# A feed-forward block with its down projection turned round: tokens stand, weight columns move

## Chip, cores and metric

The kernel runs on one core of a Trainium2 chip. The metric is the device time of one execution in microseconds (us); less is better. The number given is the median of several executions.

## What is computed

One layer of a hybrid decoder for 320 tokens (256 of a new sequence, 8 x 8 of running ones), width 2048. Two token mixers (an mLSTM and an HGRN2) are merged and projected, and a feed-forward block follows. Inputs and weights are fp32. The part that matters here:

```
x1 = LayerNorm(alpha * x + mix)                      # alpha = 2 ** 0.25
hid = square(relu(x1 @ w_up))                        # w_up (2048, 8192)
y  = LayerNorm(alpha * x1 + hid @ w_down)            # w_down (8192, 2048)
```

The recurrent states of both mixers are outputs too.

## The kernel before

**Split products.** Every fp32 operand is split into a high half (the value rounded to the matmul's fp32r format, a ScalarE copy) and a low half (the rest, a VectorE subtraction). A product is three matmuls into one PSUM bank: high x high, high x low, low x high.

**Tiles and units.** All large projections have one form: a tile is 128 output columns; its weights stand in the array (128 x 128 pieces) and the 320 tokens move past them. A tile of 2048 input rows comes in two units of 1024 rows (`UNITS`), each one load of 512 KB into one of three raw buffers (`wr`), one ScalarE instruction for the high half and one VectorE instruction of 128 x 1024 for the low half (`prep`, L520). Halves lie in buffers `wh`/`wl` (three pairs), from the output projection on in four more that lie in tile `bb`. A unit gives TensorE 8 x 3 = 24 matmuls of 320 columns. Results are transposed: channels on partitions, tokens along the row.

**Order.** `tile_list` fixes the order of the tiles. The feed-forward part goes in four rounds f: 16 tiles "up" (2048 hidden channels), then 16 tiles "dn" that multiply these by their 2048 rows of `w_down`; each dn tile is added to `acc` (`ev_dn`, L2070, L2073). Up tiles of round 0 start before the first LayerNorm is known: they use unnormalised x1 and `ev_up` corrects the result afterwards (L2052, L2054), while `x1` (L2023, L2024) writes the normalised rows; in the first dn round `xs_` splits these for the later up rounds (L1778 into `xl`). Hidden channels are split into `bah`/`bal`.

**Who decides what runs when.** The program is written out by a planner (`Sched`): each chain of work is a generator, and the planner keeps one clock per engine, with a cost for each instruction, and emits the next instruction of the most urgent chain that would be ready. So the order on each engine is fixed when the program is built; on the chip an engine waits, in that order, for semaphores. All loads and stores but a few go over SP's queue.

**Last norm and end.** Sums over channels are matmuls with ones (`ln_add`, `total`, `ln_final`), since channels lie on partitions. After the last dn tile `y` normalises 16 tiles of 128 x 320 (L2090, L2097, one ScalarE instruction each) and stores them, while TensorE makes the final states (`m_C`: 48 matmuls of 512 columns; `h_S`: 16 products of 256 columns) from copies that POOL's queue and SP's queue bring back from memory.

Of the kernel before, what the change touches and what calls it, by code (L numbers as in the profile page):

```python
# [39 lines left out]
def tile_list():  # L40
# [34 lines left out]
UNITS = [(i, half) for i in range(FIRST, len(TILES)) for half in range(2)]  # L75
# [215 lines left out]
PE_T = 112.0  # L291
PE_4 = 400.0
# [40 lines left out]
class Program:  # L333
    def __init__(self, tc, nc, d, pools):
# [16 lines left out]
        self.f2 = p.tile([128, 5204], F32, name="f2")  # L351
        self.f3 = p.tile([128, 5120], F32, name="f3", tag="f3")
        self.rx = p.tile([128, 4096], F32, name="rx", tag="rx")
# [28 lines left out]
    def carve(self):  # L382
# [28 lines left out]
        X = Part(self.rx)  # L411
        self.cb = Pool([C(512) for _ in range(6)] + [X(512) for _ in range(8)])
# [36 lines left out]
    def carve_h(self):  # L449
# [7 lines left out]
        rxb = self.pool.tile([128, 4096], F32R, name="rxb", tag="rx")  # L457
        X, R, V, W, Z = self.Part(rxb), self.Part(self.ra), self.Part(self.ra), self.Part(rxb, 2880), self.Part(rxb, 3840)
        self.nc.gpsimd.memset(rxb[:, 3840:4096].bitcast(F32), 0.0)
        self.halves = Pool([(V(512), V(512), W(448), W(448))])  # L460
        self.vp = Pool([V(256), rxb[:, 2624:2880]])
        self.ats = Pool([(Z(128), Z(128))])
        self.bah = Slices([(X if j < 12 else R)(TOK) for j in range(KT)])
# [8 lines left out]
    def carve_m(self):  # L472

        f3 = self.pool.tile([128, 5120], F32, name="f3m", tag="f3")
        self.acc = self.mm_ = self.Part(f3).three(KT, TOK)
        self.ln[0]["z"], self.ln[1]["z"] = self.mm_, self.acc

    def carve_x(self):

        self.sx = []  # L480
        for name, n in (("xh", 6), ("xl", 2)):
            R = self.Part(self.pool.tile([128, KT * (TOK + 2)], F32, name=name + "s", tag=name))
            self.sx += [R(768) for _ in range(n)]

    def carve_o(self):
        R = self.Part(self.pool.tile([128, 4096], F32, name="oC", tag="rx"))
        self.oC = [R.three(2, 512) for _ in range(MH)]
        self.oS = self.Part(self.pool.tile([128, 6656], F32, name="oS", tag="ra")).three(HH, 256)
# [12 lines left out]
    def prep(self, must=False):  # L501

        u = self.next_prep
        if u >= len(UNITS) or not self.hl_free:
            return False
        now = self.s.t["pe"]
        if must:
            self.s.until(lambda: u in self.raw_at)
        elif u not in self.raw_at:
            return False  # L510
# [1695 lines left out]
```

## Time and profile before

| | |
|---|---|
| median of 3 runs | 2276.83 us (2276.64 to 2277.16) |
| profiled execution, span | 2275.6 us, 39057 instructions |
| TensorE (PE) busy | 2267.5 us, 100% |
| VectorE (DVE) busy | 1392.1 us, 61% |
| ScalarE (ACT) busy | 1170.8 us, 51% |
| moved by DMA | 424.95 MB, 187 GB/s |

The span is the time between the first and the last instruction of the profiled execution; the median of the runs lies 1.2 us above it. "PE" are matmuls, "PEld" the loading of the standing operand, which overlaps them; "PEclk" is the clock granted to TensorE, in tenths of full speed or as a fraction. Matmuls are pipelined: one of 320 columns is listed with some 309 ns, but the next starts sooner. In lists of groups the columns are line, engine, operation, tiles, shapes and count, then busy us and mean ns, then idle time before them and what ended it. In an order of time the columns are start, duration, what.

### The profile page before, as it was taken

To read this page: it belongs to the slowest core of one execution; us is meant where nothing else is said; L and a number is where in the kernel's file an instruction comes from. 1 tells how busy PE (TensorE), PEld (TensorE's weight loads), DVE (VectorE), ACT (ScalarE), POOL (GpSimd) and SP (SyncE) were. 2 spreads that over 40 slices of the span, in tenths; PEclk is the share of its full clock that TensorE was granted. 3 is DMA by queue.
4 is the path that set the end of the run, shared out by engine and by line. 5 is a ranking of instruction groups with operands and counts; after the bars stand their busy time and mean duration, and the time that the engine had idled before them with its cause. 6 is when DMAs were issued, how large, how long until landed. Compare 5 with 4: busy or idle time off the path is not lost.

```text
span 2275.6 us, 39057 instructions
## 1 busy us (share of the span) xinstructions
PE 2267.5 (100%) x15518; PEld 2230.4 (98%) x15518; DVE 1392.1 (61%) x2426; ACT 1170.8 (51%) x2081; POOL 12.5 (1%) x36
## 2 busy tenths in 40 slices
PE   9999999999999999999999999999999999999998
PEld 9999999999999999999999999999999999999998
DVE  5676777777777777666555767544444444444456
ACT  6566555678777766444433446533432343234334
POOL 0000000000000000000000000000000000000000
PEclk9999999999999999999999999999999999999999
DMA  7588898666666575555556544444444444444476
GB/s 283 175 266 253 277 285 248 211 191 189 188 195 211 178 216 175 175 173 172 172 173 198 193 153 147 148 150 151 153 148 148 149 151 153 150 148 148 150 229 194
DMA packets 227438, 424.95 MB, mean 187 GB/s; under 512 B 96436, under 2 KB 122932, under 8 KB 226232
## 3 DMA queue, kind: packets, MB, share of 16 engines
q1 hardware_dynamic: 222376, 415.98, 56.9%
q0 software_dynamic: 4736, 6.29, 1.2%
q8 instruction: 121, 1.98, 0.4%
q14 instruction: 61, 0.50, 0.1%
q10 hardware_dynamic: 144, 0.20, 0.0%
HBM read 371.49 MB, written 50.90 MB: 186 GB/s over the span
## 4 chain that ended last, share of the span: by engine, by line
PE 97%; ACT 2%; DVE 0%; issue 0%; ACTq 0%; POOL 0%; DVEq 0%; POOLq 0%
PE bank L375 97%; ACT f L369 1%; ACT wh L369 0%; ACT f3m L369 0%; ACT ra L369 0%; ACT oC L369 0%; DVE f3m L2090 0%; DVE f3m L2097 0%; DVE wl L520 0%; ACT oS L369 0%; ACT xh L369 0%; ACTq L2202 0%; ACT f3h L369 0%; DVE f L1975 0%; DVE f L1974 0%
## 5 line engine op out<-in xcount | busy, mean ns | idle before, releaser
L520 DVE TENSOR_TENSOR wl<-wr,wh 128x1024 fp32r<-128x1024 f32 x440 | 538.8, 1225 | 432.3 <-ACT wh L369 429.2
L375 PE MATMUL bank<-xh,wh 128*128 128x320 f32 (+1 forms) x2504 | 786.5, 315 | 0.0
L375 PE MATMUL bank<-xh,wl 128*128 128x320 f32 (+1 forms) x2504 | 774.4, 310 | 0.0
L375 PE MATMUL bank<-xl,wh 128*128 128x320 f32 (+1 forms) x2504 | 772.1, 309 | 0.0
L369 ACT ACTIVATE wh<-wr 128x1024 fp32r<-128x1024 f32 x440 | 465.4, 1058 | 456.1 <-PE bank L375 437.0
L375 PEld LDWEIGHTS bank<-xh,wh 128*128 128x128 f32 x2504 | 471.2, 188 | 9.2 <-issue 7.3
L375 PEld LDWEIGHTS bank<-xl,wh 128*128 128x128 f32 x2504 | 471.3, 188 | 3.0
L375 PEld LDWEIGHTS bank<-xh,wl 128*128 128x128 f32 x2504 | 471.6, 188 | 0.2 <-DVE wl L520 0.2
L369 ACT ACTIVATE bb<-wr 128x1024 fp32r<-128x1024 f32 x162 | 171.6, 1059 | 296.0 <-PE bank L375 276.0
L520 DVE TENSOR_TENSOR bb<-wr,bb 128x1024 fp32r<-128x1024 f32 x162 | 198.5, 1225 | 195.2 <-ACT bb L369 195.0
L375 PE MATMUL bank<-ra,wh 128*128 128x320 f32 x1008 | 276.2, 309 | 0.7 <-DVE ra L1778 0.7
L375 PE MATMUL bank<-ra,bb 128*128 128x320 f32 x1096 | 255.5, 309 | 0.0
L375 PE MATMUL bank<-xh,bb 128*128 128x320 f32 (+1 forms) x1136 | 253.8, 309 | 0.0
L375 PE MATMUL bank<-rxb,bb 128*128 128x320 f32 x1088 | 249.1, 309 | 0.0
L375 PEld LDWEIGHTS bank<-xh,bb 128*128 128x128 f32 x1136 | 191.0, 188 | 0.0
L375 PE MATMUL bank<-rxb,wl 128*128 128x320 f32 x608 | 187.9, 309 | 0.0
L375 PE MATMUL bank<-rxb,wh 128*128 128x320 f32 x608 | 187.9, 309 | 0.0
L375 PEld LDWEIGHTS bank<-ra,bb 128*128 128x128 f32 x1096 | 185.2, 188 | 0.0
L375 PEld LDWEIGHTS bank<-rxb,bb 128*128 128x128 f32 x1088 | 184.6, 188 | 0.0
L375 PEld LDWEIGHTS bank<-ra,wh 128*128 128x128 f32 x1008 | 181.3, 188 | 0.9 <-DVE ra L1778 0.9
L375 PE MATMUL bank<-xl,bb 128*128 128x320 f32 (+1 forms) x568 | 175.5, 309 | 0.0
L369 ACT ACTIVATE f<-f 32x128 f32<-32x128 f32 (+6 forms) x405 | 150.7, 373 | 37.1 <-DVE f L1343 19.0
(274 smaller groups left out, 2257.3 us busy)
## 6 DMA issues: line engine op xcount, KB each, us to landing
wr<-wt SPq DMA_DIRECT2D x602, 512.0 KB, 3.4
rx<-C SPq DMA_DIRECT2D x36, 256.0 KB, 5.1
Cs<-rx SPq DMA_DIRECT2D x36, 256.0 KB, 4.5
f<-C SPq DMA_DIRECT2D x28, 256.0 KB, 4.7
Cs<-f SPq DMA_DIRECT2D x28, 256.0 KB, 5.5
f<-first SPq DMA_DIRECT2D x6, 704.0 KB, 9.6
vD<-ra SPq DMA_DIRECT2D x4, 1024.0 KB, 6.5
f<-S SPq DMA_DIRECT2D x8, 512.0 KB, 5.1
```

What stands on the lines that cost most here:

```text
L369: return self.nc.scalar.activation(out, in_, func, **kw)
L375: self.nc.tensor.matmul(*a, **kw)
L520: self.V().tensor_tensor(lo, raw, hi.bitcast(F32), ALU.subtract)
```

## The change

- `tile_list` gives 64 up tiles in eight phases of eight tiles (1024 hidden channels each) and no dn tiles. `unit_list` puts a phase's down units between the up units of the next phase (`merge`): phase 0 starts with five down units, a later one with one; the last phase has down units alone.
- In the down projection the hidden channels of 128 tokens stand and 512 weight columns move. A phase has four pairs of 128 rows; `g` is a half of the 2048 output columns. Phases 0 to 6 use a seven-product form of a 2 x 2 block product (tokens 0-127 and 128-255, the two row blocks of a pair, the two column blocks of a half): unit A and B make 10 matmuls, C 9, into three banks each (`PASSES`). The last 64 tokens stand with high and low halves side by side, two matmuls instead of three. The last phase is plain (units D and E, 16 matmuls each).
- `highs` and `lows` replace `prep` from the first down unit on. B adds two weight blocks, C forms three sums from two loads and has a third block of halves. A down unit's weights are loaded once for A or B and again for C: 8 x 4 x 7 loads for A, B and C, 16 for D and E. `refill` hands a raw buffer to the next load; `carve_dn` adds a fourth raw buffer, in the scratch tile of the first norm.
- `ev_up` leaves hidden channels in fp32, `operands` makes the differences (`Z`) and splits them. `ev_block` keeps 18 blocks of 128 x 512 and adds each phase to them; `residual` combines these after phase 6 and adds alpha * x1, which `spill_x1` has transposed and stored after phase 0's start.
- Tokens now lie on partitions, so the last norm takes its statistics along rows (`ev_last`, `norm`); gain and bias are loaded as rows. The output is stored as 12 pieces of up to 128 x 512, and the states in 16 stores.
- Buffers `rx`, `f2` and others are cut differently.

```
-    for f in range(4):
-        t += [("up", j, f, "w_up", 0, (f * 16 + j) * 128) for j in range(16)]
-        t += [("dn", j, f, "w_down", f * D, j * 128) for j in range(16)]
+    t += [("up", j, j // 8, "w_up", 0, j * 128) for j in range(8 * PH)]
     return t
...
+PH, PAIRS = 8, 4
...
+def merge(down, up, lead):
+    out, rest = down[:lead], down[lead:]
+    for n, u in enumerate(up):
+        out.append(u)
+        out += rest[len(rest) * n // len(up):len(rest) * (n + 1) // len(up)]
+    return out if up else down
+def unit_list():
+    w = lambda lo, hi: [("w", i, half) for i in range(lo, hi) for half in range(2)]
+    u = w(FIRST, UP0 + 8)
+    for p in range(PH):
+        kinds = "ABC" if p < PH - 1 else "DE"
+        down = [(k, p, g, i) for g in range(2) for k in kinds for i in range(PAIRS)]
+        u += merge(down, w(UP0 + 8 * p + 8, UP0 + 8 * p + 16) if p < PH - 1 else [], 1 if p else 5)
+    return u
...
+RAWS = dict(w=(None,), A=(0,), B=(1,), C=(0, 1), D=(0,), E=(1,))
...
+PASSES = dict(
+    A=((0, "a", 0), (1, "b", 512), (2, "s", 0), (2, "t", 512)),
+    B=((0, "z7", 0), (1, "z3", 512), (2, "s", 0), (2, "sd", 512)),
+    C=((0, "z5", 0), (1, "d", 512), (2, "z6", 1024)),
+    D=((2, "s", 0), (2, "t", 512), (0, "a", 0), (0, "b", 512), (1, "c", 0), (1, "d", 512)),
+)
+PASSES["E"] = PASSES["D"]
+PARTS = dict(A="AS", B="BS", C="C", D="ASC", E="ASC")
...
+    def carve_dn(self):
+        now = self.s.t["pe"]
+        B = self.Part(self.pool.tile([128, 5204], F32, name="f2m", tag="f2"))
+        self.m_blocks = [B(512) for _ in range(5)] + self.m3
+        self.refill(B(1024), now)
+        self.qp[1].free += [(now, B.three(2, TOK)) for _ in range(2)]
+        self.mbank.free += self.sbank.free
...
+    def refill(self, buf, at):
+        r = self.next_raw
+        if r < len(RAW_UNIT):
+            self.next_raw += 1
+            self.raw[r] = buf
+            self.s.spawn(self.reload(r, at), -2)
...
+    def highs(self):
+        v = self.nc.vector
+        for u in range(U_MLP, len(UNITS)):
+            kind = UNITS[u][0]
+            rs = RAW_OF[u]
+            yield wait(*[self.raw_ev[r] for r in rs])
+            raw = [self.raw[r] for r in rs]
+            buf = yield acq(self.hlp)
+            x = raw[0]
+            if kind == "B":
+                yield ("dve", SUM, lambda: v.tensor_tensor(x[:, 0:512], x[:, 0:512], x[:, 512:1024], ALU.add))
+            if kind == "C":
+                y = raw[1]
+                yield ("dve", SUM, lambda: v.tensor_tensor(x[:, 0:512], x[:, 0:512], y[:, 0:512], ALU.add))
+                yield ("dve", SUM, lambda: v.tensor_tensor(y[:, 0:512], x[:, 0:512], y[:, 512:1024], ALU.add))
+                yield ("dve", SUM, lambda: v.tensor_tensor(x[:, 512:1024], x[:, 512:1024], y[:, 0:512], ALU.add))
+            yield ("act", HI, lambda: self.A(buf[0], x))
+            self.half[u] = [buf, None]
+            yield post(self.hi_ev[u])
+            if kind == "C":
+                c2 = yield acq(self.c2)
+                yield ("act", act(512), lambda: self.A(c2[:, 0, :], y[:, 0:512]))
+                self.half[u][1] = c2
+                yield post(self.h2_ev[u])
+    def lows(self):
+        v = self.nc.vector
+        for u in range(U_MLP, len(UNITS)):
+            yield wait(self.hi_ev[u])
+            raw = [self.raw[r] for r in RAW_OF[u]]
+            hi, lo = self.half[u][0]
+            x = raw[0]
+            t = yield ("dve", LO, lambda: v.tensor_tensor(lo, x, hi.bitcast(F32), ALU.subtract))
+            self.refill(x, t)
+            if UNITS[u][0] == "C":
+                yield wait(self.h2_ev[u])
+                c2, y = self.half[u][1], raw[1]
+                t = yield ("dve", SUM, lambda: v.tensor_tensor(c2[:, 1, :], y[:, 0:512], c2[:, 0, :].bitcast(F32), ALU.subtract))
+                self.refill(y, t)
+            self.unit[u] = (self.half[u][0], t + LAT)
...
+    def down(self, u, kind, p, g, i):
+        s = self.s
+        if (kind, g, i) == ("A", 0, 0) and p == 0:
+            s.until(lambda: self.n_zg == 8 and all(e.t is not None for e in self.acc_ev))
+            self.carve_dn()
+            s.spawn(self.xs_(), 0)
+            s.spawn(self.spill_x1(), 4)
+        if (kind, g, i) == ("D", 0, 0):
+            self.carve_end()
+            ...
+            s.spawn(self.residual(), 1)
+        if (kind, g, i) == ("E", 1, 0):
+            for j in range(MH):
+                s.spawn(self.m_C(j), 3)
+            for j in range(HH):
+                s.spawn(self.h_S(j), 3)
+        if i == 0:
+            self.banks = [self.take() for _ in range(3)]
+        (hi, lo), at = self.halves_of(u)
+        c2 = self.half[u][1]
+        X = self.X[p, i]
+        for part in PARTS[kind]:
+            s.until(lambda: X["ev" + part].t is not None)
+            at = max(at, X["ev" + part].t + LAT)
+        s.t["pe"] = max(s.t["pe"], at)
+        passes = PASSES[kind]
+        for n, (b, name, o) in enumerate(passes):
+            wh, wl = (c2[:, 0, :], c2[:, 1, :]) if o == 1024 else (hi[:, o:o + 512], lo[:, o:o + 512])
+            x = X[name]
+            jobs = [(x[0], wh), (x[1], wh), (x[0], wl)] if len(x) == 2 else [(x[0], wh), (x[0], wl)]
+            for m, (l, w) in enumerate(jobs):
+                self.mm(self.banks[b], l, w, start=..., stop=...)
+                s.t["pe"] += 227.0
+            if i == PAIRS - 1 and n == last[b]:
+                s.spawn(self.ev_block(kind, p, g, b, self.banks[b]), 0)
+        self.give(u)
...
+    def spill_x1(self):
         v = self.nc.vector
+        for j in range(KT):
+            yield wait(self.xs_ev[j])
+            z = self.mm_[:, j, :]
+            yield ("dve", dve_t(TOK), lambda: v.transpose(z, z))
+            yield from self.place(lambda a: cap2(self.xD, 128 * j + 32 * a, [[D, 32], [32 * D, 10], [1, 32]]),
+                                  z.rearrange("p (b c) -> p b c", c=32))
+        yield wait(self.later())
+        self.carve_f3()
+        yield post(self.f3_ev)
...
+    def ev_up(self, T, p, b):
+        v = self.nc.vector
+        i, h = T % 8 // 2, T % 2
+        if h == 0:
+            self.Q[p, i] = yield acq(self.qp[p > 0])
+            yield post(self.q_ev[p, i])
+        else:
+            yield wait(self.q_ev[p, i])
+        q = self.Q[p, i][:, h, :]
+        if p:
+            yield ("act", act(TOK, True), lambda: self.A(q, b[:, :TOK], AF.Relu))
             yield rel(self.mbank, b)
+        else:
+            sm = yield acq(self.sm)
+            yield ("act", act(2, True), lambda: self.A(sm[:, 0:2], b[:, TOK:TOK + 2]))
+            yield wait(self.ln[0]["end"])
+            yield ("dve", dve(TOK, True), lambda: v.scalar_tensor_tensor(q, self.lnb[3], sm[:, 0:1], b[:, :TOK], ALU.mult, ALU.subtract))
+            yield rel(self.mbank, b)
+            yield ("dve", dve(TOK), lambda: v.tensor_tensor(q, q, self.lnb[4], ALU.mult))
+            yield ("act", act(TOK, False, 1), lambda: self.A(q, q, AF.Relu, scale=-1.0, bias=sm[:, 1:2]))
+            yield rel(self.sm, sm)
+            self.n_zg += 1
+        yield ("act", act(TOK), lambda: self.A(q, q, AF.Square))
+        yield post(self.hq_ev[T])
+        if h:
+            yield wait(self.hq_ev[T - 1])
+            yield from self.operands(p, i)
...
+    def operands(self, p, i):
...
+        if not plain:
+            Z = yield acq(self.zp)
+            yield ("dve", dve(256), lambda: v.tensor_tensor(two(Z, 0, 128, 128), two(flat, 0, 128, 128), two(flat, 128, TOK, 128), ALU.subtract))
+            yield ("dve", dve(128), lambda: v.tensor_tensor(Z[:, 384:512], Z[:, 0:128], flat[:, TOK + 128:TOK + 256], ALU.add))
+            yield ("dve", dve(128), lambda: v.tensor_tensor(Z[:, 256:384], Z[:, 384:512], flat[:, TOK:TOK + 128], ALU.subtract))
+            yield ("dve", dve(64), lambda: v.tensor_tensor(Z[:, 512:576], flat[:, TOK + 256:2 * TOK], flat[:, 256:TOK], ALU.subtract))
+        A = X["A"] = yield acq(self.pA)
+        yield from halves(two(A, 0, 128, 128), two(A, 256, 128, 128), two(flat, 0, TOK, 128), 256)
+        X["a"], X["b"] = (A[:, 0:128], A[:, 256:384]), (A[:, 128:256], A[:, 384:512])
+        yield post(X["evA"])
...
+    def ev_block(self, kind, p, g, b, bank):
+        v = self.nc.vector
+        if kind in "DE":
+            yield from self.ev_last("DE".index(kind), g, b, bank)
             return
+        if p == 0 and 9 * g + 3 * "ABC".index(kind) + b >= 8:
+            yield wait(self.f3_ev)
+        M = self.block(kind, g, b)
+        if p:
+            yield ("dve", dve(512, True), lambda: v.tensor_tensor(M, M, bank, ALU.add))
+        else:
+            yield ("act", act(512, True), lambda: self.A(M, bank))
+        yield rel(self.mbank, bank)
+        if p == PH - 2:
+            yield post(self.sum_ev[kind, g, b])
...
+    def residual(self):
...
+            yield wait(*[self.sum_ev[k, g, b] for k in "ABC" for b in range(3)])
+            blocks = ((P2, P3), (Q4, P7), (S1, S2))
+            yield tt(P2, P1, P2, ALU.add)
+            yield tt(P1, P1, Q6, ALU.subtract)
+            yield tt(Q6, P1, P7, ALU.add)
+            yield tt(Q4, Q4, Q6, ALU.add)
+            yield tt(Q5, Q5, P1, ALU.subtract)
+            yield tt(P3, Q5, P3, ALU.subtract)
+            yield tt(P7, Q5, P7, ALU.subtract)
+            for n in range(2):
+                c = 2 * g + n
+                for x in range(3):
+                    yield ("dve", SUM, lambda: v.scalar_tensor_tensor(w, e, ALPHA, w, ALU.mult, ALU.add))
+                    yield post(self.w_ev[c][x])
...
+    def ev_last(self, n, g, x, bank):
+        v = self.nc.vector
+        c = 2 * g + n
+        W = self.last(c, x)
+        yield wait(self.w_ev[c][x])
+        yield ("dve", dve(512, True), lambda: v.tensor_tensor(W, W, bank, ALU.add))
+        yield rel(self.mbank, bank)
+        rows = 128
+        if x == 2:
+            t = yield acq(self.ts)
+            rows = 64
+            yield ("act", act(512), lambda: self.A(t[0:64], W[64:128]))
+            yield ("dve", SUM, lambda: v.tensor_tensor(W[0:64], W[0:64], t[0:64], ALU.add))
+            yield rel(self.ts, t)
+        yield ("dve", SUM, lambda: v.bn_stats(self.st[:rows, x, c, :], W[:rows]))
+        yield post(self.s_ev[x, c])
+        if c == 3 and x != 0:
+            yield from self.norm((2,) if x == 2 else (0, 1))
...
+    def norm(self, xs):
...
+        for j, x in enumerate(xs):
+            m, r = self.mv[:rows, x, 0:1], sm[:rows, 9 + n + j:10 + n + j]
+            for c in range(4):
+                W = self.last(c, x)[:rows]
+                cc = slice(512 * c, 512 * c + 512)
+                yield ("dve", SUM, lambda: v.scalar_tensor_tensor(W, W, m, G[:rows, cc], ALU.subtract, ALU.mult))
+                yield ("dve", SUM, lambda: v.scalar_tensor_tensor(W, W, r, B[:rows, cc], ALU.mult, ALU.add))
+                yield ("sp", 620, lambda: self.dma(self.d["y"][128 * x:128 * x + rows, cc], W))
```

More of the change, by code (lines that the diff above doesn't have):

```diff
@@ L474, in carve_m @@
         f3 = self.pool.tile([128, 5120], F32, name="f3m", tag="f3")
[L475 to L488, printed above, removed]
+        self.mm_ = self.Part(f3).three(KT, TOK)
@@ new lines, in carve_f3, with carve_end @@
+    def carve_f3(self):
+        m10 = self.Part(self.pool.tile([128, 5120], F32, name="m10", tag="f3"))
+        self.m_blocks += [m10(512) for _ in range(10)]
+    def carve_end(self):
+        R = self.Part(self.pool.tile([128, KT * (TOK + 2)], F32, name="xhe", tag="xh"))
+        self.erest = R.ap
+        self.er = [R(2048), R(2048), R(1024)]
+        R = self.Part(self.pool.tile([128, KT * (TOK + 2)], F32, name="xle", tag="xl"))
+        self.gb2 = [R(2048), R(2048)]
+        self.ts = Pool([R(512) for _ in range(2)])
@@ L708, in start @@
         self.zg_ev = [Ev() for _ in range(KT)]
-        self.hid_ev = [[Ev() for _ in range(KT)] for _ in range(4)]
         self.m_ev = [Ev() for _ in range(KT)]
```

429 lines of the change are left out of this document (248 added, 181 removed).

## The prediction

> **What bounds the kernel now.** I read the page first (busy shares, the slices, the chain), then the chain in order of time, then stretches of the last half, then single instructions.
>
> ```profile
> span 2275.6 us, 39057 instructions
> PE 2267.5 (100%) x15518; PEld 2230.4 (98%) x15518; DVE 1392.1 (61%) x2426; ACT 1170.8 (51%) x2081; POOL 12.5 (1%) x36
> ...
> DVE  5676777777777777666555767544444444444456
> ...
> PEclk9999999999999999999999999999999999999999
> ...
> PE 97%; ACT 2%; DVE 0%; issue 0%; ACTq 0%; POOL 0%; DVEq 0%; POOLq 0%
> ```
>
> TensorE is busy all the time at full granted clock and holds 97% of the chain. VectorE (DVE) has room, most of it in the last 900 us, which is the feed-forward part.
>
> ```profile
> 620.43 732.63 PE bank L375 x5053
> 1353.06 111.37 PE bank L375 x750
> ...
> 1468.30 783.58 PE bank L375 x5341
> ```
>
> The last piece is almost the whole feed-forward part: 783.58 / 5341 = 146.7 ns per matmul. So time is the number of matmuls times their spacing, as long as the other engines keep up:
>
> ```profile
> core 0: us, PE busy (x) PEld busy (x) DVE busy (x) ACT busy (x) POOL busy (x), PEclk, DMA share, GB/s
> ...
> 300.00:400.00 100.00, 100.00 (x685) 91.84 (x685) 78.62 (x156) 54.70 (x96) 0.00 (x0) 1.00 0.87 263
> ...
> 700.00:800.00 100.00, 100.00 (x713) 97.60 (x712) 77.20 (x181) 77.15 (x182) 0.37 (x1) 1.00 0.63 188
> ...
> 1470.05:2245.00 774.95, 774.95 (x5289) 774.95 (x5289) 363.93 (x437) 280.32 (x342) 4.87 (x7) 1.00 0.47 153
> 2252.95:2262.48 9.53, 9.53 (x44) 7.88 (x43) 8.85 (x22) 7.30 (x14) 0.00 (x0) 1.00 0.71 272
> 2269.50:2275.60 6.10, 0.04 (x1) 0.00 (x0) 0.42 (x1) 0.76 (x2) 0.00 (x0) 0.81 0.69 241
> ```
>
> VectorE 77% and ScalarE 77% busy (700 to 800 us), or 263 GB/s (300 to 400 us), still left TensorE full; the feed-forward part uses 47% of VectorE and 153 GB/s.
>
> **Matmuls.** The state products behind the last weight tile already run in the new shape, 512 moving columns of split fp32r:
>
> ```profile
> 2252.95 0.84 PE L375 MATMUL bank<-bb,wl 128*128 128x512 f32 x3
> 2253.64 2.20 PE L375 MATMUL bank<-bb,wh 128*128 128x512 f32 x9
> 2255.68 0.84 PE L375 MATMUL bank<-bb,wl 128*128 128x512 f32 x3
> ```
>
> Nine starts take 2255.68 - 2253.64 = 2.04 us: 227 ns each, at granted clock 1.00 (window 2252.95 to 2262.48). Old down projection: 4 x 16 tiles x 16 x 3 = 3072 matmuls x 146.7 = 450.7 us. New: a pair (256 rows of w_down by 1024 columns) takes 10 + 10 + 9 = 29 matmuls in the seven-product form, 7 phases x 2 x 4 x 29 = 1624; the plain phase 2 x 4 x (16 + 16) = 256. 1880 x 227 = 426.8 us: **-23.9 us**. Per pair: 7.04 us before, 6.58 after, plain 7.26, so merely turning the operands costs 3% and the missing product earns it back. The margin is 3.4 us per phase of 109 us; everything below is whether stalls eat it.
>
> The Trainium skill ("TensorE: Matmul & The Clock Gate", Back-to-back issue gap) gives N/2.4 + 2.5 ns, 216 ns for 512 columns, by which the new projection would take 405 us and the gain be 45 us. The same rule gives 136 ns for 320 columns where the trace has 146.7, so the measured 227 decides.
>
> **VectorE per phase** (16 up units with 24 down units, 384 x 146.7 + 232 x 227 = 109.0 us of TensorE). Spacing of instructions back to back:
>
> ```profile
> 1412.74 1.23 DVE L520 TENSOR_TENSOR wl<-wr,wh 128x1024 fp32r<-128x1024 f32 x1 [1.78 <-ACT wh L369]
> 1413.88 0.48 DVE L2023 TENSOR_TENSOR f3m<-f3m,f 128x320 f32<-128x320 f32 x1
> 1414.28 0.49 DVE L1778 TENSOR_TENSOR ra<-f,rxb 128x320 fp32r<-128x320 f32 x1
> ...
> L1305 DVE SCALAR_TENSOR_TENSOR rx<-rx,f,bank 128x512 f32<-128x512 f32 x36 | 25.8, 737 | 0.2
> ...
> L369 ACT ACTIVATE wh<-wr 128x1024 fp32r<-128x1024 f32 x440 | 465.4, 1058 | 456.1 <-PE bank L375 437.0 <-issue 9.6 <-DMA wr<-wt 6.9
> ```
>
> 1024 elements 1.14 us, 320 elements 0.40 us; on the line through both (an estimate) 512 take 0.60, 256 0.33, 128 0.20, 64 0.13. Low halves 40 x 1.14 = 45.6. Sums of weights (one in B, three in C, and C's third low half): 40 x 0.60 = 24.0. Adding banks: 18 x 0.65 (737 less the overlap of 0.09) = 11.7. Operands of four pairs: 4 x (4 x 0.33 + 4 x 0.20 + 2 x 0.13) = 9.5. Together 91 us, 83% of 109. ScalarE has 40 x 0.97 (1058 less the same overlap) plus smaller copies, about 60 us; it does not bind. So TensorE stays the bound on average, but not everywhere: four C units with their 2.8 up units give TensorE 4 x 2.04 + 9.9 = 18.0 us and VectorE 4 x (1.14 + 4 x 0.60) + 3.2 + 2.0 + 1.6 = 20.9 us.
>
> **Weight loads** of the down projection go from 128 to 240, on SP's queue. Issue (0.33 us each) takes 16 us of a phase there:
>
> ```profile
> wr<-wt SPq DMA_DIRECT2D x602, 512.0 KB, 3.4
> ...
> L378 SPq DMA_DIRECT2D wr<-wt x602: 327/328/2364, 9.7 to 2231.2; - x151
> ```
>
> 48 loads per 109 us are 231 GB/s, below the 263 of 300 to 400 us. Four raw buffers (three, and one more from the first down unit on) allow 4 x 109 / 48 = 9.1 us per load. A plain load holds its buffer 3.4 + 1.06 + 1.23 + hand-overs, about 6 us; C's two hold theirs about 9 us each, since three sums stand ahead of the high half. In a C stretch that is 4 x 18.5 + 2.8 x 6 = 91 buffer-us for 72 at hand: 23 us instead of 18, 5 us late, 14 times. The cover is the prepared units: five buffers of halves, four of them ahead at about 2.7 us, 10.9 us; A and B stretches (11.4 and 13.8 us of VectorE for 18.9) refill them. That units are prepared ahead until the buffers are full shows here (waits inside the feed-forward part):
>
> ```profile
> ACT bb L369 <- PE bank L375: 271.3, 128, 2.5
> ACT wh L369 <- PE bank L375: 203.7, 96, 2.5
> DVE bb L520 <- ACT bb L369: 176.4, 136, 2.9
> DVE wl L520 <- ACT wh L369: 134.4, 105, 2.9
> ```
>
> ScalarE waits for TensorE to free a buffer. I take **0** for the C stretches, bounds 0 and 14 x 5 = 70 us.
>
> **Start of the first down phase.** It now comes after 8 up tiles, not 16, and needs every operand that reads the first norm.
>
> ```profile
> 1346.10 0.31 PE L375 MATMUL bank<-xh,bb 128*128 128x322 f32 x1
> ...
> 1364.72 0.49 DVE L1976 SCALAR_TENSOR_TENSOR f<-f 128x320 f32<-128x320 f32 x1
> ...
> L2023 DVE TENSOR_TENSOR f3m<-f3m,f x16: 483/484/487, 1367.0 to 1421.0; 128x320 f32<-128x320 f32 x16
> ...
> L369 ACT ACTIVATE xh<-f3m x16: 453/456/463, 1462.0 to 1490.8; 128x320 fp32r<-128x320 f32 x16
> L1778 DVE TENSOR_TENSOR xl<-f3m,xh x16: 483/485/488, 1463.7 to 1492.1; 128x320 fp32r<-128x320 f32 x16
> ...
> 1468.30 0.41 PE L375 MATMUL bank<-ra,wh 128*128 128x320 f32 x1 [0.65 <-DVE ra L1778]
> ```
>
> The first up tile starts at 1346. The norm ends at 1365 and x1 (L2023) lasted to 1421, hidden under up tiles that ran to 1464. Eight up tiles end at 1346 + 56 = 1402. From 1367 to 1402 VectorE would have 13 us of x1, 7 of evictions, 12 of low halves and 10 of operands, 42 us for 35, plus chained waits: x1 ends near 1412. The split of x1 (16 x 0.9 us, strictly after it) delays the up units of the next phase, which follow only five down units (11.3 us) later: eight splits make 1421, so 1421 - 1402 - 11.3 = **+7.7 us**, and the old gap of 0.65 goes. Bounds: -0.65 (x1 packed tighter) and +20 (x1 at its old pace to 1421, splits behind it). SP's queue waits there too: the fourth raw buffer lies in the norm's scratch, so its first load stands until x1 is done, with the other weight loads behind it; five units of halves are ready by then and cover that. Behind that, 16 transposes and 64 small stores of x1 must end before the ninth block is evicted, some 50 us on; banks give slack for 30 us more. I take **+3**, bounds 0 and 15.
>
> **Tail.**
>
> ```profile
> L1069 DVE BATCH_NORM_STATS2 misc<-f 128x6 f32<-128x512 f32 x12 | 8.3, 688 | 0.9 <-ACT f L369 0.8
> ...
> 2250.46 0.86 PE L375 MATMUL bank<-bb,wh 128*128 128x512 f32 x3
> ...
> 2266.52 1.69 DVE L2097 TENSOR_TENSOR f3m<-f3m,f 128x320 f32<-128x320 f32 x4
> ...
> 2267.65 1.89 PE L375 MATMUL bank<-xls 128*128 128x256 f32 x8
> ...
> 2270.78 0.95 SPq L378 DMA_DIRECT2D Sp<-oS  x2
> ```
>
> Now the last tile ends at 2250.5 and the program 25.1 us later: VectorE 18 us, TensorE's state products 19. Afterwards the same 48 + 16 state products stay; VectorE adds the last bank and two before it and takes their statistics (0.65 + 0.60 each; about 2.5 us are left after the last matmul), forms the root (some seven short instructions and two of ScalarE, taken as 2 us), then 24 instructions of 0.60 = 14.4: 19 us. The outputs go in 28 stores instead of 21 (7 more issues, 2.3 us of SP beside that). The plain phase before it (58.1 us of TensorE) holds 51 us of VectorE: 16 low halves 18.2, the residual 26 x 0.60, twelve additions and statistics with four folds, 17.4. State products' operands come over POOL's queue into buffers freed by the last five units; the order of the state products leaves them 8 us and more. I take **0**, bounds -3 and +5.
>
> **Sum** against the execution's span: 2275.6 - 23.9 - 0.65 + 7.7 + 3 = 2261.8; the median stands 1.2 us above that span (2276.83): **2263**.
>
> **Rivals.**
> 1. Everything hides: start and spill cost nothing. 2276.8 - 24.5 = 2252. For: before, the gap at the same seam was 0.65 us. Against: x1 ended 19 us after the new seam.
> 2. VectorE waits on ScalarE (slower). Before each low half VectorE sat idle 310.8 us / 241 = 1.29 us. Alternating with ScalarE, it keeps some of that idle. The work of a phase is 91 us and about 4 of gaps between dependent sums; at 0.5 us idle for each of 40 units a phase takes 91 + 4 + 20 = 115 instead of 109, +42 over seven: 2263 + 42 = 2305. It decides once the remaining 14 us are gone, 2 us per phase, at 0.4 us idle per unit. For: 83% load, and C above 100%. Against: 77% on both engines together left TensorE full (700 to 800 us), so most idle is slack, not need.
> 3. The C stretches break through in part, 1 us each: 2263 + 14 = 2277, no change.
>
> The clock can fall in the gaps: it reads 0.81 in the idle last 6.10 us, which is worth 0.19 x 6.1 = 1.2 us per gap. The Trainium skill (same page, Part 1) halves it after an idle window of 3.4 us; no gap inside the old feed-forward part was that long, so no run here shows it there.
>
> **How the numbers follow.** Forecast (2256 to 2272) 0.50; all hidden 0.18; no change 0.12; VectorE bound 0.20. Range 2250 to 2300: it leaves out the worse half of the last case and little else; the forecast's own range is 2256 to 2272. A measurement of this kernel tells about 0.2% (2272 to 2281) from no change: faster 0.68, same 0.12, slower 0.20.
>
> **What would show it.** The 512-column matmuls 227 ns apart at clock 1.00; in steady phases VectorE busy 83 to 90% and TensorE full at 109 us per phase, 231 GB/s; TensorE gaps of 4 to 12 us after the eighth up tile, ended by x1's split; a tail of 22 to 30 us. The forecast is wrong if TensorE's waits name a low half of a C unit or a weight load again and again, if the first down phase lasts over 130 us, or if the spacing is not 227 ns.

## Result and the profile after

The kernel became slower: 2340.79 us (2339.35 to 2341.54) against 2276.99 us, a ratio of 1.0279 [1.0264, 1.0294]. The forecast was 2263 us, the range ended at 2300. The profiled execution has a span of 2339.8 us, 64.2 us over the one before.

The page after, its lines that answer to those of before:

```profile
span 2339.8 us, 37835 instructions
PE 2286.6 (98%) x14316; PEld 2142.6 (92%) x14316; DVE 1697.1 (73%) x2982; ACT 1280.9 (55%) x2339; POOL 12.6 (1%) x36
...
DVE  6676677777677876565556688777877787777776
...
PE 24%; DVE 7%; DMA 4%; ACT 3%; issue 2%; SPq 0%; POOL 0%; DVEq 0%; ACTq 0%; POOLq 0%
```

There are 1202 matmuls fewer (1192 in the down projection, and ten with `ones`). The chain can be followed back only to 1411 us here, so its shares add up to some 40% of the span: of the last 929 us TensorE holds some 557 (24% of the span), and loads, VectorE and ScalarE have come into it. The same view in order of time (start, duration, what; some of the longest pieces of one phase) shows where:

```profile
1645.20 41.67 PE bank L411 x231
1693.40 1.24 DVE wl L660
1694.65 3.44 DMA wr<-wd
1703.08 33.81 PE bank L411 x187
1739.44 3.55 DMA wr<-wd
1749.15 3.42 DMA wr<-wd
1762.43 43.22 PE bank L411 x231
```

Before, TensorE held one piece of 783 us. Now it holds some 40 us, the units A and B of a half with their up units, and then the chain leaves it for 16 to 26 us: the C units. By phases (from the first up unit of one to that of the next), behind a row of the start and ahead of one of the tail:

```profile
core 0: us, PE busy (x) PEld busy (x) DVE busy (x) ACT busy (x) POOL busy (x), PEclk, DMA share, GB/s
1403.00:1441.00 38.00, 32.89 (x147) 26.16 (x146) 32.63 (x62) 24.00 (x47) 0.00 (x0) 0.91 0.64 170
1528.73:1649.26 120.53, 114.24 (x617) 101.35 (x616) 92.39 (x137) 57.47 (x88) 0.00 (x0) 0.97 0.64 210
1649.26:1768.03 118.77, 113.61 (x617) 100.75 (x616) 94.63 (x142) 58.74 (x91) 0.00 (x0) 0.99 0.65 217
...
2316.34:2321.60 5.26, 5.26 (x13) 4.10 (x13) 5.12 (x9) 0.60 (x1) 0.00 (x0) 0.50 0.85 317
```

A phase takes 119 to 121 us instead of 109.0, with VectorE busy 92 to 95 us of it. What TensorE waited for between 1530 and 2230 (us in total, times, longest) are halves of units, high and low:

```profile
PE bank L411 <- ACT bb L405: 20.0, 12, 3.4
PE bank L411 <- DVE bb L660: 7.6, 15, 0.5
```

The row of 2316 is in the tail; it is read below.

**Ledger.** From the first up matmul to the last matmul on a weight tile the kernel took 904.4 us before (1346.1 to 2250.5) and takes 953.6 now (1346.0 to 2299.6): +49.2. The tail behind it was 25.1 us and is 40.2: +15.1. The 49.2 are made of -23.9 (matmuls, as forecast at 227 ns), +10.5 (their spacing is 233 ns), some +10 at the start (1402 to 1445) and some +55 behind it, in the C stretches. "Lost" here and below is the length of a stretch less what its matmuls, counted in the trace, need at 147 and 233 ns. Of the 55, 45.5 are in the five phases from 1528.73 to 2125.74, each 9.1 us over what a phase takes with no waits (110.3 us; experiment 3 shows that figure); 2.6 lie before them and 6.4 behind. This adds up to some 52; the ten matmuls with `ones`, which are gone, take off 1.5.

**One C stretch**, second half of phase 2. The chain of waits between 1739 and 1763:

```profile
1739.44 3.55 DMA wr<-wd
...
1743.08 0.69 DVE wr L640
1743.78 0.60 DVE m L2320
1744.37 0.60 DVE wr L641
1744.98 1.19 DVE m L2320 x2
1746.17 0.61 DVE wr L642
...
1746.81 1.07 ACT wh L405
...
1747.90 1.22 DVE wl L660
...
1749.15 3.42 DMA wr<-wd
...
1761.15 1.24 DVE bb L660
...
1762.43 2.75 PE bank L411 x6
```

A load lands; three sums (with additions of banks, L2320, between them), the high half on ScalarE, the low half on VectorE; only then is the buffer given to the next load, which goes out at 1749.15, 9.7 us after the one before. Each link waits for the last. VectorE, in the stretch that was thought its tightest, stands idle for the load:

```profile
1743.08 0.69 DVE L640 TENSOR_TENSOR wr<-wr 128x512 f32<-128x512 f32 x1 [1.46 <-DMA wr<-wd]
...
1752.67 0.69 DVE L640 TENSOR_TENSOR f2m<-f2m,wr 128x512 f32<-128x512 f32 x1 [1.27 <-DMA wr<-wd]
```

The pace is read from the copies into `c`, one for each C unit (minimum/median/maximum ns, first and last start):

```profile
L405 ACT ACTIVATE c<-wr x4: 616/617/621, 1738.2 to 1761.3; 128x512 fp32r<-128x512 f32 x4
```

Three steps in 23.1 us: 7.7 us for each C unit. TensorE needs 9 x 0.233 + 0.7 x 24 x 0.147 = 4.57 us for a C unit with its share of up units (16 stand between 23 down units). So four of them make 4 x (7.7 - 4.57) = 12.5 us of delay. The cover, TensorE's lead at the end of B, was some 8 us: the last B unit has its low half (list of VectorE) ready at 1733.52 + 1.23 = 1734.75, and TensorE takes it up (list of TensorE) at 1742.58:

```profile
1733.52 1.23 DVE L660 TENSOR_TENSOR bb<-wr,bb 128x1024 fp32r<-128x1024 f32 x1 [0.51 <-ACT bb L405]
```

```profile
1742.58 1.57 PE L411 MATMUL bank<-bb,xp 128*128 128x512 f32 x6
...
1757.22 1.21 PE L411 MATMUL bank<-bb 128*128 128x512 f32 x4 [0.51 <-DVE bb L660]
1758.27 0.99 PE L411 MATMUL bank<-c,bb 128*128 128x512 f32 x3
1761.17 0.73 PE L411 MATMUL bank<-bb 128*128 128x512 f32 x2 [1.91 <-ACT bb L405]
1762.43 1.90 PE L411 MATMUL bank<-bb 128*128 128x512 f32 x4 [0.53 <-DVE bb L660]
```

By the third C unit the lead is gone and TensorE waits for each half as it is made. 12.5 - 8 = 4.5 us a stretch, two stretches a phase: 9 us, the loss seen. That it fits so closely is in part luck. The waits of this stretch are 0.51 + 1.91 + 0.53 = 2.95 us, since TensorE begins with a unit's high half before the low half is done (1761.17 and 1762.43); most of the rest is the granted clock, which reads 0.50 from 1762.7 to 1766.1, just behind them. Low clock is in the loss everywhere: 0.97 to 0.99 over the five phases is worth some 12 of the 45.5 us.

### The profile page after: what moved, and what is told of

Same layout as the page of the kernel before. It is cut to its first block, busy times and chain, and to the rows that moved or that the text cites. A ratio compares the mean times of both kernels' runs of the same rounds, so it can differ in the third digit from the quotient of the medians.

```text
span 2339.8 us, 37835 instructions
## 1 busy us (share of the span) xinstructions
PE 2286.6 (98%) x14316; PEld 2142.6 (92%) x14316; DVE 1697.1 (73%) x2982; ACT 1280.9 (55%) x2339; POOL 12.6 (1%) x36
## 5 line engine op out<-in xcount | busy, mean ns | idle before, releaser
L411 PEld LDWEIGHTS bank<-xl,wh 128*128 128x128 f32 x2776 | 522.7, 188 | 11.4 <-DVE xl L1984 4.7
L660 DVE TENSOR_TENSOR bb<-wr,bb 128x1024 fp32r<-128x1024 f32 x89 | 108.8, 1222 | 52.8 <-ACT bb L405 52.5
L405 ACT ACTIVATE f<-f 32x256 f32<-32x256 f32 (+6 forms) x339 | 120.7, 357 | 35.9 <-DVE f L1550 19.0
L411 PE MATMUL bank<-xh,bb 128*128 128x320 f32 (+1 forms) x592 | 136.2, 310 | 0.0
L411 PE MATMUL bank<-ra,wh 128*128 128x320 f32 x468 | 128.3, 309 | 0.0
L411 PE MATMUL bank<-wh,xp 128*128 128x512 f32 x336 | 118.1, 402 | 0.0
L411 PE MATMUL bank<-bb,wh 128*128 128x320 f32 (+1 forms) x524 | 116.7, 312 | 0.0
L411 PE MATMUL bank<-bb 128*128 128x512 f32 x294 | 86.3, 420 | 30.6 <-ACT bb L405 21.7
L411 PE MATMUL bank<-bb,xp 128*128 128x512 f32 x416 | 104.2, 396 | 0.0
L411 PEld LDWEIGHTS bank<-xh,bb 128*128 128x128 f32 x592 | 100.6, 188 | 1.5 <-DVE bb L660 0.2
L411 PE MATMUL bank<-wl,xp 128*128 128x512 f32 x232 | 92.7, 400 | 0.0
```

The source lines that it names most:

```text
L405: return self.nc.scalar.activation(out, in_, func, **kw)
L411: self.nc.tensor.matmul(*a, **kw)
L660: t = yield ("dve", LO, lambda: v.tensor_tensor(lo, x, hi.bitcast(F32), ALU.subtract))
```

## The experiments

Theory 1: the load buffers pace the C stretches, because a C unit holds two of the four from the load to its low halves. Theory 2: VectorE, with more work than TensorE in a C stretch, does. "Expected" is the text written before the run. Experiments 1 to 6, 10 and 12 are one execution each, 7, 8, 9 and 11 medians of 4, 4, 5 and 11.

**1. Three load buffers.**

```
-        self.refill(B(1024), now)
+        B(1024)
```

> Three buffers for weight loads instead of four (the one in f2m is never handed out); nothing else changes. Theory 1 (buffers): four C units and 2.8 up units hold their load buffers for some 91 buffer-us; over three buffers this is 30 us a stretch, over four 23, against 18 of TensorE, so 14 stretches lose about 7 us more each: 2440 us (2400 to 2490), phases of some 133 us instead of 119.4. Theory 2 (VectorE has 20.9 us of work for 18 of TensorE, and waits for ScalarE in it): VectorE's work is the same; 2341 us, within 10.

2494.14 us. The five phases from 1550.65 and, in one of their C stretches, the copies into `c`:

```profile
1550.65:2246.95 696.30, 605.64 (x3082) 523.01 (x3080) 477.79 (x691) 292.07 (x441) 1.03 (x1) 0.92 0.55 182
```

```profile
L405 ACT ACTIVATE c<-wr x4: 613/616/617, 1655.6 to 1682.8; 128x512 fp32r<-128x512 f32 x4
```

139 us a phase and some 9 us for each C unit, with VectorE's busy time hardly changed (95.6 us a phase). Theory 2 alone is out. The time is just above theory 1's range (2490), so the estimate by buffer-us was too mild here too. The ledger of one stretch holds here as well: over the ten C stretches of these five phases the low halves of C units end 9.5 us apart and TensorE's lead at the end of B is 5.9 us, 4 x (9.5 - 4.57) - 5.9 = 13.8, and (139.3 - 110.3) / 2 = 14.5 us were lost in each. (In the changed kernel the same means are 7.7 and 8.2 us, which gives 4.3; 4.6 were lost.)

**2. Six load buffers**, taken from the prepared ones (five to four).

```
+        if n == 1 and u >= U_MLP - 6:
+            for x in hl:
+                self.refill(x, now)
...
+        if self.raw[r].dtype == F32R:
+            t = yield ("pool", 1000, lambda: self.nc.gpsimd.dma_start(self.raw[r], self.raw_source(r)), (at,))
...
```

> Six buffers for weight loads: one of the five buffers of prepared weights becomes two load buffers, filled through POOL's queue; sums written into those two are rounded. Four buffers of prepared weights stay. Theory 1: 91 buffer-us over six are 15 us, less than the 18 of TensorE; the stretches of C stop waiting, phases of 110.5 to 113 us instead of 119.4, and the time is 2285 us (2275 to 2305). Theory 2: the same as after or a little over, 2338 to 2355, since one prepared unit less is a shorter cover.

2311.50 us: 29 us of the loss came back, more than theory 2 allows and less than theory 1 said. Five phases, and what TensorE waited for in them (us in total, times, longest):

```profile
1531.93:2099.33 567.40, 556.84 (x3082) 498.33 (x3080) 464.25 (x693) 289.62 (x447) 41.87 (x80) 1.00 0.68 223
```

```profile
PE bank L411 <- DVE wl L665: 7.1, 10, 0.9
PE bank L411 <- ACT wh L405: 3.5, 5, 0.7
```

113.5 us a phase. C units now follow each other by 6.2 to 6.4 us, but with one prepared unit less the lead at the end of B is 4.8 us in the first half of a phase and 6.3 in the second, and 4 x (6.3 - 4.57) = 6.9 is just over it. Nor is it the rate of transfers that limits: 223 GB/s here is more than the 210 to 217 of the changed kernel, and experiment 11 moves 230 GB/s with TensorE full.

**3. One load for a C unit.** The second weight block is left out of the sums; their number and size stay, so the kernel computes something else with the same work on VectorE and eight loads a phase fewer.

```
-RAWS = dict(w=(None,), A=(0,), B=(1,), C=(0, 1), D=(0,), E=(1,))
+RAWS = dict(w=(None,), A=(0,), B=(1,), C=(0,), D=(0,), E=(1,))
...
```

> C units load one weight block instead of two (the second block is left out of the sums; number and size of the sums, copies and subtractions stay). Theory 1: a C stretch holds some 53 buffer-us, 13 a buffer, so its waits go: phases of 110.5 to 113 us, 2287 us (2275 to 2305). Theory 2: VectorE has the same work, 2335 us or more (2325 to 2345, the little being the wait for the second transfer).

2284.95 us, as theory 1 said (2287). Five phases:

```profile
1525.97:2077.32 551.35, 551.35 (x3081) 499.77 (x3080) 461.71 (x688) 286.72 (x439) 1.03 (x1) 1.00 0.59 191
```

TensorE is busy for all of the 551.35 us: a phase with no waits takes 110.3 us. VectorE has the same instructions as after, 92.3 us of a phase, 84%. It can bear them. Its own pace shows too:

```profile
L405 ACT ACTIVATE c<-wr x3: 615/616/623, 1721.6 to 1740.6; 128x512 fp32r<-128x512 f32 x3
L405 ACT ACTIVATE c<-f2m x1: 618/618/618, 1728.4 to 1728.4; 128x512 fp32r<-128x512 f32 x1
```

Four units from 1721.6 to 1740.6, 6.3 us each. That is over TensorE's 4.57 as well: 7 us a stretch, just inside the cover of 8. VectorE's waits between these four are 3.0 us for ScalarE's high halves and 0.6 for TensorE, none for a load, and with six buffers (experiment 2) the pace was 6.3 too. So VectorE and the hand-overs to ScalarE set a floor of 6.3; the two-load buffers raise it to 7.7, and only that passes the cover.

**4. No additions on VectorE.** ScalarE copies the banks in every phase; the sum over the phases is left out.

```
-        if p:
-            yield ("dve", dve(512, True), lambda: v.tensor_tensor(M, M, bank, ALU.add))
-        else:
-            yield ("act", act(512, True), lambda: self.A(M, bank))
+        yield ("act", act(512, True), lambda: self.A(M, bank))
```

> Banks of the down projection are copied by ScalarE in every phase instead of being added by VectorE (the sum over the phases is left out): 18 additions of 0.6 us, 11 us of 91, leave VectorE in each phase after the first. Theory 1: only the additions that stand in a C stretch's chain between a load's landing and the buffer's release go, at most 1.9 us in each of 14: 2315 to 2338 us. Theory 2: VectorE has 11 us more room a phase, which is the whole of the loss: 2260 to 2300 us.

2317.13 us, in theory 1's range at its lower end. VectorE lost 10 us a phase, but a phase fell by only 4 (577.18 us for five, 115.4):

```profile
L405 ACT ACTIVATE c<-wr x4: 616/617/623, 1733.9 to 1755.8; 128x512 fp32r<-128x512 f32 x4
```

7.3 us for each C unit: 4 x (7.3 - 4.57) - 8 = 2.9 us a stretch, and (115.4 - 110.3) / 2 = 2.6 was lost. What VectorE does between a load's landing and the buffer's release counts; its total does not.

**5. The tail, and the order of the seven products.**

```
-        if (kind, g, i) == ("E", 1, 0):
+        if (kind, g, i) == ("E", 0, 0):
...
+        elif self.sx_early and buf.dtype == F32:
+            self.sx.free.append((at, buf[:, 0:768]))
...
+            self.vx.free.append((s.t["pe"], self.c2all))
...
-            jobs = [(x[0], wh), (x[1], wh), (x[0], wl)] if len(x) == 2 else [(x[0], wh), (x[0], wl)]
+            jobs = [(x[0], wh), (x[0], wl), (x[1], wh)] if len(x) == 2 else [(x[0], wh), (x[0], wl)]
```

> Two edits, read apart. The tail: the buffers for the state loads come free earlier (the c2 tile serves as a further value buffer, load buffers that have no further weight to load serve for the state products, and the chains of the last products are spawned half a pass earlier). If the tail's 15 us over the forecast are waits for these loads, the time from the last matmul on a weight tile to the end falls from 40 us to 27 (24 to 31); if it is the work itself it stays at 38 to 41. The spacing: in each seven-product block the order is hi x hi, hi x lo, lo x hi, so that the same stationary serves two matmuls running. If a change of the stationary costs the 6 ns over 227, the spacing falls to 228 to 230 ns and 5 to 9 us go in the body; if not it stays at 233. Together 2328 us (2316 to 2336); 2341 if neither holds.

2329.06 us. The tail fell from 40.2 to 26.9 us, as expected (2300.36 to 2327.3); the spacing stayed at 233 ns, so the order of the products is not what makes it 233 (the standing operand is loaded for each matmul in either order: 14316 loads for 14316 matmuls). The list of TensorE in the changed kernel's tail shows what the 15 us were:

```profile
2304.70 1.03 PE L411 MATMUL bank<-bb,wl 128*128 128x512 f32 x3 [2.12 <-DMA bb<-vD]
2305.53 1.48 PE L411 MATMUL bank<-xp 128*128 128x512 f32 x3
...
2316.34 5.46 PE L411 MATMUL bank<-xp,wh 128*128 128x512 f32 x12 [4.32 <-DMA xp<-vD]
...
2332.37 3.44 PE L411 MATMUL bank<-xhe 128*128 128x256 f32 x8 [5.00 <-DMA xhe<-iD]
```

Three waits for state loads, 11.4 us: each load could start only when an earlier product had freed its buffer. The rest is the clock: in the row of 2316.34 to 2321.60 it reads 0.50, and 12 matmuls took 5.26 us, 438 ns each instead of 227. With buffers that come free earlier and chains that start half a pass earlier (one edit; the two were not parted) one short wait is left, and the 256-column products follow at once:

```profile
2303.70 0.93 PE L411 MATMUL bank<-bb,wl 128*128 128x512 f32 x3 [1.08 <-DMA bb<-vD]
...
2316.26 3.62 PE L411 MATMUL bank<-xhe 128*128 128x256 f32 x16
```

**6. Up units where they are needed.**

```
+    out, k, acc = [], 0, 0.0
+    w = dict(A=0.25, B=0.5, C=1.25) if lead == 1 else dict(A=0.125, B=0.125, C=1.875)
+    for n, x in enumerate(down):
+        acc += 0.0 if lead > 1 and n < 8 else w.get(x[0], 0.0)
+        while acc > 0.999 and k < len(up):
+            out.append(up[k])
+            k, acc = k + 1, acc - 1.0
+        out.append(x)
...
```

> The up units stand 1.25 after each C unit, 0.5 after each B and 0.25 after each A, instead of evenly (the first phase: none before its first eight down units, 1.875 after each C). A C stretch then has 5 up units and some 26 us of TensorE for 104 buffer-us, 26 over four buffers. Theory 1: the waits go or nearly so, phases of 110.5 to 113 us, and the start loses less than its 8 us: 2285 us (2272 to 2300). If it were not the pace of loads in the C stretch but something that each C unit pays wherever it stands (its chain of load, three sums, two copies, two subtractions), phases stay at 118 to 121 us and the time at 2330 or more.

2304.48 us: 36 us less, so most of the C waits went, and a C unit's own chain is no fixed toll. It missed its range (to 2300) all the same: ahead of 1530 us it lost 20 us instead of 13, and some 9 us were still lost in the phases up to 2235.

**7 and 8. Order and tail, with four and with six load buffers.** The edits of 5 (without its order of products) and 6; then that of 2 as well.

> The spread of the last kernel with the earlier buffers of the tail (order of the seven products as in the changed kernel). Theory 1 with the tail: 2272 us (2258 to 2290), at or just under the kernel before; else 2330.

> The same with six load buffers and four of prepared weights. If load buffers still bind in the spread order, 3 to 10 us less than the last kernel; if four buffers are enough there, the same or a few us more, since the cover is a prepared unit shorter and two buffers are filled through POOL's queue: 2270 us (2256 to 2292).

2303.50 us (1.0111 [1.0094, 1.0128]) and 2285.59 us (1.0038 [1.0023, 1.0053]). The first is a miss: its tail was 26.9 us, but its last weight tile came 12 us later than in experiment 6 (9.5 us of waits between 1515 and 2235 against 3.2, of up to 1.6 us each); why it lost more there with the same order I did not find out. With six buffers the waits of the phases were gone and the last weight tile ended at 2250.2, where the kernel before had it. Load buffers bound the spread order too.

**9 and 10. The split of x1 in two chains**, with six buffers (and one more value buffer for the state loads) and with four.

```
-            s.spawn(self.xs_(), 0)
+            s.spawn(self.xs_(0), 0)
+            s.spawn(self.xs_(1), 0)
...
```

> The last kernel (spread order, earlier buffers of the tail, six load buffers) with two edits: the 16 splits of x1 run as two chains of eight instead of one of sixteen, and the two added load buffers become a value buffer for the state loads when they are done. If the 13 us of gaps at the start are the length of one chain (ScalarE, then VectorE, 16 times one behind the other), they fall to some 5; if VectorE is full there (18 us busy of 20), they stay. The tail, 32 us because the fourth value buffer was late, falls to 27. 2272 us (2264 to 2282) where both hold, under the kernel before by 5; 2281 where only the tail does.

> The spread kernel with the earlier tail and four load buffers, and the splits of x1 in two chains as above; this parts the start from the load buffers. One chain as the cause: 16 us of gaps between 1400 and 1510 fall to some 8, 2295 us (2288 to 2300). VectorE full there, or the load buffers: 2303 us as without the edit (2300 to 2306).

2285.73 us (1.0037 [1.0024, 1.0051]) and 2303.68 us: no gain, both missed. TensorE's waits between 1400 and 1515, first without and then with two chains (four buffers):

```profile
PE bank L416 <- DVE xl L1993: 5.7, 8, 1.3
PE bank L416 <- ACT m L410: 3.2, 2, 3.0
...
```

```profile
PE bank L416 <- ACT m L410: 15.6, 1, 15.6
...
```

The waits for the split did go, so one chain of 16 was their cause. TensorE then ran into the next one some 55 us later: copies of banks into blocks that come free only when x1 has been spilled. The gain was more than given back as one wait of 15.6 us (9.5 with six buffers): all waits of these 115 us went from 11.5 to 19.7 us, with six buffers from 9.2 to 14.9. The times stayed because less was lost behind 1530 (four buffers) and in the tail (six).

**11. The even order in the first phase alone**, the rest as 9, value loads ahead of key loads.

```
+    if lead > 1:
+        out, rest = down[:lead], down[lead:]
...
+    w = dict(A=0.25, B=0.5, C=1.25)
```

> The version with six load buffers, the earlier tail and two chains for the splits of x1, with the first phase in the even order of the changed kernel (the spread order only from the second phase on) and the value loads of the state issued ahead of the key loads. In the spread first phase the banks' copies waited 9.7 us for blocks that come free when x1 is spilled; in the even order this wait should not come: gaps of 5 us at the start instead of 17, and 2.8 us less in the tail. 2272 us (2266 to 2282); 2285 if the spill binds in any order.

2275.80 us, 0.9993 [0.9984, 1.0002]: the same as before, 65 us under the changed kernel. The chain has one long piece again:

```profile
1524.56 712.01 PE bank L422 x3911
```

Its last weight tile ends at 2247.6 (2250.5 before) and its tail is 26.5 us (25.1). The time is in its range; the waits at the start (1400 to 1515) are still 8 us, not 5, and with the clock 12 us are lost there.

**12. Address of the standing operand.**

```
-        self.f2 = p.tile([128, 5204], F32, name="f2", tag="f2")
+        self.f2 = p.tile([128, 5212], F32, name="f2", tag="f2")
...
```

> The changed kernel with f2 eight columns (32 bytes) longer, so that the tiles behind it, among them the products xp, c and rh that stand in the down projection, begin at the same address modulo 64 as the weights that move. Products in xp, c and rh now go at 233 to 235 ns a matmul, those in bb at 228 to 231. If the address of the stationary is the cause, xp's matmuls fall to 228 to 230 and the time by 4 to 8 us: 2334 us (2331 to 2338); if not, the spacing stays 233 and the time 2341 (2338 to 2344).

2344.90 us; the mean spacing went from 232.7 to 231.8 ns, a sixth of what was to be explained, and the time is 0.9 us over the range that went with no effect. So the address modulo 64 is not the cause. The shift did change the spacing by operands (matmuls that read `c` and `bb` went from 233.9 to 230.0 ns, those that read `xp` fell by 1 to 2), so another effect of where operands lie is not ruled out.

## Why the prediction was wrong, step by step

- **The step that failed: weight loads, "I take 0 for the C stretches", of 0 to 70.** The mechanism was named and bounded; the sum took the wrong end. Two numbers in it were off. A stretch was to need 23 us of supply (5 us late); it needs 4 x 7.7 = 31 (12.5 late). Buffer-us were shared out as if any buffer could serve any load; in fact a C unit needs two at once, in the order of the units, and gives them back only through load, sums, high half and low half one after the other. And the cover was taken as four units at 2.7 us, 10.9; it was 8, since A and B stretches are also used to catch up: the lead is 1.4 us at the first A unit of the half shown (low half done at 1707.11, first matmul at 1708.56) and 7.8 at its last B unit. With the two measured numbers the same working gives 12.5 - 8 = 4.5 us, 14 times 63; some 55 were lost.
- **Clock.** It was named, at 1.2 us a gap, and left out of the sum. It makes some 12 of the 45.5 us that five phases lost.
- That units are prepared ahead "until the buffers are full" was read from rows of before, where each unit had one load and no sums. That supply of 128 loads said nothing about 240.
- **Spacing.** 227 ns came from 44 matmuls of the state products in the tail. The 512-column matmuls of the down projection stand 233 ns apart (229 to 235 by operands), with the clock at 1.00; two rows of the list of TensorE, ten starts in 2294.53 - 2292.19 = 2.34 us:

```profile
2292.19 2.50 PE L411 MATMUL bank<-bb,xp 128*128 128x512 f32 x10
2294.53 1.55 PE L411 MATMUL bank<-bb 128*128 128x512 f32 x6
```

  1880 x 5.6 ns = 10.5 us of 23.9. The trace of before had the larger figure as well: 49 matmuls of 512 columns ahead of the feed-forward part (standing operand `ra`) stand 233 ns ahead of the next matmul, on average. And the state products themselves, 227 ns in the tail of before, stand 232 ns apart in experiment 5's. So it is not the down projection as such. Order of the products and the address shift of experiment 12 do not explain it, nor does traffic (232.4 ns with no transfer in flight). The cause stays open. The back-to-back rule of the Trainium skill's "TensorE: Matmul & The Clock Gate", 216 ns, is further off than 227 was.
- **Tail.** Taken as 0 (-3 to +5) and measured +15.1, outside its bounds. VectorE was not what ended the program; "the order of the state products leaves them 8 us and more" was not: three loads were late, since their buffers were in use by the products ahead (POOL's queue waited 12.7 us for TensorE before it issued the one that landed at 2316).
- **Start.** +7.7 forecast, some 10 measured: 5.1 us of waits between 1400 and 1445, of which 4.2 for the split of x1 as said, and low clock behind them (0.66 from 1420 to 1430). The spill, +3 forecast, cost nothing that shows in this order: experiment 3 has it too and loses nothing between 1441 and 1526.
- **VectorE.** 91 us a phase forecast, 92.3 with no waits (experiment 3). The slow rival, VectorE waiting on ScalarE, named the right sign for another reason: the waits that count are for buffers, and with the same VectorE work and one load for a C unit TensorE is full. The pace of C without that limit, 6.3 us, is a fifth over the 20.9 / 4 = 5.2 of the sum: the hand-overs.
- The sign that was to show it wrong, TensorE waiting "again and again" for halves of C units, is what the trace shows.

Without the waits of the C stretches the change would be worth little: -23.9 + 10.5 + 10 at the start leaves 3 us. Experiment 11 shows it: its last weight tile ends 2.9 us earlier than before, its tail is 1.4 us longer, and it comes out even.

## What to carry to other kernels

A loop of buffers is costed by its own cycle, from one load's landing to the next load's issue, along the order in which units need them; dividing the sum of holding times by the number of buffers is too mild where one unit needs two at once. Compare that cycle with the consumer's for the worst run of units, and set the difference times the run's length against the measured lead; here 4 x (7.7 - 4.57) - 8 gave the loss, and with pace and lead measured in each run the same formula fits the runs with three and six buffers, with one load and without additions, low clock included. Where cover is near its limit, spread the light units between the heavy ones before looking for memory; and look at what the stretch behind a removed wait will run into, since the split in two chains gave its gain back within 60 us.

## What the runs showed of the hardware

- 512-column fp32r matmuls went at 227 ns in the tail of before and at 233 ns (226 to 238) in the new projection, at the same granted clock, whatever the order of the products (experiment 5); those of the state products went at 232 ns in experiment 5's tail. 320-column ones kept a median of 147 ns.
- Short waits can cost clock as well as time: in the tail the matmuls after a wait of 2.12 us (from 2305.53) stood some 0.42 us apart, and after one of 4.32 us the clock read 0.50 and 12 matmuls took 5.26 us instead of 2.7. The Trainium skill ("TensorE: Matmul & The Clock Gate", Part 1) has the clock halve after an idle window of some 3.4 us; here a wait of 2.12 us was enough. It is not the length of a wait alone: in the tail of experiment 8 (2250 to 2257) the clock read 1.00 before and behind one of 2.95 us. In the steady phases, with waits of up to 3.4 us, the clock read 0.97 to 0.99, so TensorE was "busy" for 114 us of a phase that takes 110.3 at full clock.
- A load queue on POOL (experiment 2, 80 loads in 567 us) fed TensorE as well as SP's: POOL was busy 42 us of these, and with the spread order no wait was left that it could have caused.
